# Both mixers' value products in plain float32, two 64-column halves at a time, in bursts

## The chip, the cores and the metric

The kernel runs on one core of one Trainium2 chip. The metric is the device time of one execution in microseconds (us). TensorE (PE) multiplies matrices into PSUM banks of 128 x 512 float32; VectorE (DVE), ScalarE (ACT) and GpSimd (POOL) do the rest, and SyncE (SP) issues most DMAs. Each engine works through its own queue in order.

## The reference, cut to what matters

One layer of a hybrid backbone: 1024 latent tokens and 128 context tokens of width 1024. One projection gives queries, keys, values and gates for two mixers of 8 heads of 64, with 2 key/value groups each. Mixer A attends from every latent token to all 1024 latent and 128 cached context keys. Mixer B attends to a window of +-128 tokens and the cached context, with a sink logit in the softmax. The context tokens attend to themselves.

```python
# mixer A, one block of 128 queries (k_all, v_all: 128 context + 1024 latent)
s = jnp.einsum('bqkgd,bskd->bkgqs', qblk, k_all).astype(jnp.float32) * (d ** -0.5)
p = jax.nn.softmax(s, axis=-1).astype(v_all.dtype)
o = jnp.einsum('bkgqs,bskd->bqkgd', p, v_all)
...
# mixer B: the same over [sink, context, band of three blocks], the sink's weight dropped
o = einsum('bnkgqs,bskd->bnqkgd', p_ctx, v_ctx) + einsum('bnkgqs,bnskd->bnqkgd', p_band, vband)
...
out = jnp.concatenate([o_a * jax.nn.silu(g_a), o_b * jax.nn.silu(g_b)], axis=-1) @ w_out
xs = xs + gate * out
```

Everything is float32. The kernel reaches that accuracy on TensorE by splitting an operand into a high part in the type float32r and a low part (the rest), and adding the products of the parts.

## The kernel before, in words

The first part of the kernel (to about 300 us of the profile) normalises, modulates, projects and stores queries and gates in DRAM; keys and values stay in SBUF. The change touches there only how values are stored: `put_values` casts them to a high part `v_hi`, and `split_values` makes low parts by subtraction.

The rest is attention and the output projection, written as one loop over *slots* (L1365). A unit is (t, m, g): a block of 128 queries, a mixer (m = 0 is A, 1 is B) and a key/value group; its tile holds 4 heads x 128 queries = 512 columns. Units come as A, B, A, B for t = 1 to 8, then four context units (t = 0). A latent A unit has nine blocks of 128 keys, a B unit three or four; each block is one slot. So a *pair* (an A unit and the B unit behind it) has 12 or 13 slots. A context unit has one block and one empty slot. In every slot the program emits, in this order:

- `tick()`: what `later(n, f)` put down n slots before;
- `scores`: for A two products into a bank of tag B, which has two banks (L1217, L1218), an exp on ACT into `pe` (L1220), a cast to the high part `ph` (L1221) and the low part `pl` by subtraction on POOL, for one block in nine on DVE (L1225, L1223). For B the weights are already normalised exps in natural layout; four transposes turn them (L1212), ACT casts the high part (L1213), DVE subtracts (L1214);
- `due` items: the maxima of a later A unit (products L941, reductions on DVE, at most two a slot), and in the first four slots of an A unit the scores of the B unit behind it (L998, L999), a masked minimum with its read-out on DVE (L1002) and an exp on ACT in the next slot (L988). The negated maxima `m_nat` are transposed (L960) and written by DVE into the rows 64 to 67 of `qb` (L961), which L1218 of the next A unit reads;
- in the first four slots of all, 24 late gate products (L1146);
- products of the output projection from the queue `outq` (L1313), as many as the rate allows (`OUTRATE`, a slot); 24 for each latent pair, 36 for each context pair;
- `values` of the block that is `LAG` = 3 slots old: for A three products into the bank `pv`, for B two:

```python
nc.tensor.matmul(pv, two, ph, start=(b == 0), stop=False)                 # L1235
if m == 0:
    nc.tensor.matmul(pv[0:64, :], vl, ph, start=False, stop=False)        # L1237
nc.tensor.matmul(pv, two, pl, start=False, stop=last)                     # L1238
```

`two` is 128 columns wide: 64 columns of high values and, for A, 64 columns of ones, so the softmax's sums land in partitions 64 to 127; for B the second 64 columns are the low values. After a unit's last block, at the slots in `END_AT`, `LAST_END` or `PROMPT_END`, `inverse` makes 1/sum on ACT as exp(-ln) (A) or copies the second half (B, L1247), `gated` multiplies or adds the halves on DVE (two instructions, L1259) and multiplies with the gate `sgl` on POOL (L1261), `parts` splits the result into `ogh` (ACT, L1271) and `ogl`, and behind a B unit the pair's output products join `outq`. For B the gate `sgl` has been multiplied with 1/sum before, on POOL (L1045). `load_gate` fetches a unit's gate two units ahead. `in_order` keeps each engine's instructions in the order in which the program emits them.

Of the kernel before, what the change touches and what calls it, by code (L numbers as in the profile page):

```python
# [36 lines left out]
LAG = 3  # L37
# [93 lines left out]
def hybrid_step(ctx, tc, x_prompt, x_sample, cache_k_a, cache_v_a, cache_k_b, cache_v_b,  # L131
# [631 lines left out]
    v_hi = kv.tile([P, 2, 20, 2, HD], F32R, name="v_hi")  # L763
    v_lo = kv.tile([P, 20, HD], F32R, name="v_lo")
# [7 lines left out]
    def split_values(src, j):  # L772

        nc.vector.tensor_tensor(v_lo[:, j : j + 2, :], src[:, 0], v_hi[:, 0, j : j + 2, 0, :], op=ALU.subtract)
        nc.vector.tensor_tensor(v_hi[:, 1, j : j + 2, 1, :], src[:, 1], v_hi[:, 1, j : j + 2, 0, :], op=ALU.subtract)

    with tc.tile_pool(name="kt", bufs=2) as kt:
        W_GB.pools[WRAW : WRAW + 2] = [(kt, 2)] * 2
        sg_tile.append(lambda n: kt.tile([P, 512], F32, tag="kh", name=n))
        for b in range(0, 20, 4):  # L780
            later(4 + b // 2, lambda b=b: nc.gpsimd.tensor_scalar(
                v_hi[:, 0, b : b + 4, 1, :], gain4, 0.0, 1.0, op0=ALU.mult, op1=ALU.add))
        ones = ident_r.bitcast(F32)[64:68].unsqueeze(1)
        for out, n in ((kla[64:68].rearrange("p g b n -> p (g b) n"), 18), (klp[64:68, 0:2], 2)):
            later(ONES_AT, lambda out=out, n=n: nc.vector.tensor_scalar(
                out, ones.to_broadcast([4, n, P]), 0.0, 1.0, op0=ALU.mult, op1=ALU.add))
# [40 lines left out]
        def put_values(src, t):  # L827
            j = 2 * t if t else 18
            nc.scalar.copy(v_hi[:, :, j : j + 2, 0, :], src)
            later(1, lambda: split_values(src, j))  # L830
# [50 lines left out]
        later(VC_AT, lambda: nc.scalar.copy(v_hi[:, :, 0:2, 0, :], vc))  # L881
        later(VC_AT + 1, lambda: split_values(vc, 0))
# [295 lines left out]
    def blocks(t, m, g):  # L1178

        if t == 0:  # L1180
            k = (khp[:, g, :], klp[0:68, g, :]) if m == 0 else 0
            return [(k, v_hi[:, m, 18 + g], v_lo[:, 18 + g, :])]
        if m == 0:
            return [((kha[:, g, b, :], kla[:, g, b, :]), v_hi[:, 0, 2 * b + g], v_lo[:, 2 * b + g, :]) for b in range(9)]
        p0, p1_ = window(t)
        at = {p: b + 1 for b, p in enumerate(POS)}
        return [(p - p0, v_hi[:, 1, 2 * at.get(p, 0) + g], None) for p in range(p0, p1_)]
# [5 lines left out]
    def load_gate(i):  # L1193
        if i < NU:
            t, m, g = units[i]
            sgl[i] = w2.tile([P, 2, P], F32, tag="sgl", name=f"sgl{i}")
# [4 lines left out]
    def parts_tiles(i, b):  # L1201
        return [w3.tile([P, 512], F32R, tag=n, name=f"{n}{i}_{b}") for n in ("ph", "pl")]

    def scores(i, b, blk):
# [3 lines left out]
        ph, pl = parts_tiles(i, b)  # L1208
        if m == 1:
# [3 lines left out]
            nc.scalar.copy(ph, s)  # L1213
            later(1, lambda: nc.vector.tensor_tensor(pl, s, ph, op=ALU.subtract))  # L1214
            return ph, pl
# [3 lines left out]
        pe = w3.tile([P, 512], F32, tag="pe", name=f"pe{i}_{b}", bufs=PES)  # L1219
        nc.scalar.activation(pe, s, AF.Exp)  # L1220
        nc.scalar.copy(ph, pe)  # L1221
        if (i - PROMPT_AT in PROMPT_PL) if t == 0 else b in PL_DVE:
            later(1, lambda: nc.vector.tensor_tensor(pl, pe, ph, op=ALU.subtract))  # L1223
        else:
            nc.gpsimd.tensor_tensor(pl, pe, ph, op=ALU.subtract)  # L1225
        return ph, pl

    def values(i, b, last, blk, ph, pl):
        t, m, g = units[i]
        _, vh, vl = blk  # L1230
        if b == 0:
            pvb[i] = bank(PROMPT_PV[i - PROMPT_AT] if t == 0 else "C", f"pv{i}")
        pv = pvb[i]
        two = vh.rearrange("p s d -> p (s d)")
        nc.tensor.matmul(pv, two, ph, start=(b == 0), stop=False)  # L1235
        if m == 0:
            nc.tensor.matmul(pv[0:64, :], vl, ph, start=False, stop=False)  # L1237
        nc.tensor.matmul(pv, two, pl, start=False, stop=last)  # L1238
        if not last:
            return  # L1240

        v = {}

        def inverse():
            v["rs"] = w2.tile([64, 512], F32, tag="rs", name=f"rs{i}", bufs=1)
            if m == 1:
                nc.scalar.copy(v["rs"], pv[64:128, :])  # L1247
                return
            nc.scalar.activation(v["rs"], pv[64:128, :], AF.Ln)
            nc.scalar.activation(v["rs"], v["rs"], AF.Exp, scale=-1.0)  # L1250

        def gated():
            rs = v["rs"]
            o = 768 + 256 * (i % 3)
            of = spare[0][:, o : o + 256].rearrange("p (c n) -> p c n", c=2)
            pvv = pv[0:64, :].rearrange("p (c s n) -> p c s n", s=2, n=P)
            srv = rs.rearrange("p (c s n) -> p c s n", s=2, n=P)
            for s in range(2):
                nc.vector.tensor_tensor(of[64 * s : 64 * s + 64], pvv[:, :, s, :], srv[:, :, s, :],  # L1259
                                        op=ALU.add if m else ALU.mult)  # L1260
            nc.gpsimd.tensor_tensor(of, of, sgl.pop(i), op=ALU.mult)  # L1261
            later(GATE_LATE, lambda: load_gate(i + 2))
# [13 lines left out]
        ends = PROMPT_END if t == 0 else END_AT if i < PROMPT_AT - 2 else LAST_END  # L1276
        for n, f in zip(ends, (inverse, gated, parts)):
            later(n, f)
        if m == 1:
            later(ends[3], lambda: outq.extend(out_items(t, g)))  # L1280
# [81 lines left out]
    credit, live = 0.0, []  # L1362
    load_gate(0)
    load_gate(1)
# [86 lines left out]
```

## Time and profile before

| | |
|---|---|
| time, median of 3 runs | 704.2 us (704.17 to 704.34) |
| span of the profiled execution | 704.1 us; the page gives no other time for it |
| PE busy | 691.6 us, 98% |
| DVE, ACT, POOL busy | 443.3, 420.0, 342.3 us |
| mean granted TensorE clock | 0.997 |

In the rows that follow, L-numbers are lines of the kernel. A row of a group of instructions reads: line, engine, operation, out<-in, shapes and count, then busy us and mean ns of one, then idle time of the engine before them and what ended it. A matmul's shape is written rows*columns of the weights, then the moving operand. A row in order of time has its start and length in us first. Lengths of matmuls overlap, because they are pipelined.

### The profile page before, as it was taken

Reading aid. Unit: us, or ns where it says so; the run is one execution under the profiler, and the core shown is the slowest. Engines: PE = TensorE matmul, PEld = TensorE weight load, DVE = VectorE, ACT = ScalarE, POOL = GpSimd, SP = SyncE. Lnnn points to the kernel's source line nnn. Section 1 sums busy time; section 2 is a strip of 40 time slices with the busy share of each in tenths; the row PEclk is TensorE's granted clock in tenths of the full one; section 3 lists DMA queues with packets and bytes.
Section 4 is the critical chain, followed back from the end, with each engine's and each line's share of the span. In section 5 each row is a group of like instructions: output and inputs, shape, how many; then the busy total and the mean of one; then the engine's idle time right before and its main releaser. Section 6 shows DMA issues by size and latency. Waiting matters only on the chain.

```text
span 704.1 us, 10711 instructions
## 1 busy us (share of the span) xinstructions
PE 691.6 (98%) x3554; PEld 561.4 (80%) x3554; DVE 443.3 (63%) x991; ACT 420.0 (60%) x856; POOL 342.3 (49%) x364
## 2 busy tenths in 40 slices
PE   6999999999999999999999999999999999999997
PEld 2788988878788789986788888878888888887876
DVE  3555247875676873537677577667666775775564
ACT  4455411412233553389877877787788778877870
POOL 3457023332323241657857655755574557456742
PEclk9999999999999999999999999999999999999999
DMA  8960283348435015423222122121211231212324
GB/s 330 415 245 16 109 305 76 72 93 295 131 89 175 1 61 187 157 64 102 90 69 83 34 82 73 46 82 58 86 61 52 69 90 46 83 52 90 91 60 144
DMA packets 53447, 78.64 MB, mean 112 GB/s; under 512 B 6848, under 2 KB 25728, under 8 KB 52368
## 3 DMA queue, kind: packets, MB, share of 16 engines
q1 hardware_dynamic: 45360, 66.28, 27.8%
q10 hardware_dynamic: 8032, 11.68, 6.2%
q8 instruction: 28, 0.46, 0.3%
q14 instruction: 27, 0.22, 0.1%
HBM read 58.72 MB, written 19.21 MB: 111 GB/s over the span
## 4 chain that ended last, share of the span: by engine, by line
PE 88%; ACT 4%; DMA 2%; DVE 2%; issue 2%; ACTq 1%; SPq 0%; POOL 0%; DVEq 0%; POOLq 0%
PE po L1313 14%; PE pv L1238 6%; PE pv L1235 6%; PE pmx L941 5%; PE st L1217 4%; PE pv L1237 4%; PE st L1218 4%; PE pq L279 4%; PE pq L280 4%; PE pq L278 4%; PE st L1212 4%; PE pg L292 3%; PE pg L293 3%; PE pg L288 3%; PE pk L279 2%; PE pk L280 2%
## 5 line engine op out<-in xcount | busy, mean ns | idle before, releaser
L1225 POOL TENSOR_TENSOR pl<-pe,ph 128x512 fp32r<-128x512 f32 x130 | 167.9, 1294 | 141.9 <-DVE nm L1002 67.5
L942 DVE TENSOR_REDUCE mx<-pmx 128x1 f32<-128x384 f32 x192 | 101.4, 553 | 57.3 <-PE pmx L941 56.2
L1220 ACT ACTIVATE pe<-st 128x512 f32<-128x512 f32 x146 | 86.7, 594 | 27.1 <-PE st L1218 26.4
L1221 ACT CAST ph<-pe 128x512 fp32r<-128x512 f32 x146 | 90.6, 621 | 4.8
L1238 PE MATMUL pv<-pl,v_hi 128*128 128x512 f32 x208 | 82.5, 397 | 0.3 <-POOL pl L1225 0.3
L1235 PE MATMUL pv<-ph,v_hi 128*128 128x512 f32 x208 | 82.6, 397 | 0.0
L197 POOL TENSOR_TENSOR rs_q<-ms_q,mhalf 128x8 f32<-128x8 f32 x18 | 34.8, 1931 | 80.7 <-DVE ms_q L195 80.7
L1313 PE MATMUL po<-wo,ogh 128*128 128x512 f32 (+1 forms) x224 | 73.1, 387 | 0.0
L1002 DVE CUSTOM_DVE_ANT_0 sn<-sn,mask,nsink 128x512 f32<-128x512 f32 (+1 forms) x64 | 46.4, 724 | 41.0 <-PE sn L999 38.6
L941 PE MATMUL pmx<-kha,qt 128*128 128x384 f32 x192 | 61.0, 363 | 0.5 <-ACT pen L988 0.3
L1217 PE MATMUL st<-qt,kha 128*128 128x512 f32 x144 | 57.9, 402 | 0.1
L1237 PE MATMUL pv<-ph,v_lo 128*64 128x512 f32 x146 | 57.6, 395 | 0.0
L1218 PE MATMUL st<-qb,kla 68*128 68x512 f32 x144 | 57.1, 397 | 0.0
L1238 PEld LDWEIGHTS pv<-pl,v_hi 128*128 128x128 f32 x208 | 39.2, 188 | 17.3 <-POOL pl L1225 0.7
L988 ACT ACTIVATE pen<-sn,nm 128x512 f32<-128x512 f32 (+2 forms) x72 | 44.9, 625 | 5.8 <-DVE nm L1015 2.7
L1213 ACT CAST ph<-st 128x512 fp32r<-128x512 f32 x62 | 36.4, 587 | 19.7 <-PE st L1212 19.4
L1313 PEld LDWEIGHTS po<-wo,ogh 128*128 128x128 f32 x224 | 41.0, 188 | 6.2 <-ACT ogh L1271 0.3
L1235 PEld LDWEIGHTS pv<-ph,v_hi 128*128 128x128 f32 x208 | 39.3, 189 | 7.0 <-issue 0.3
L1313 PE MATMUL po<-wo,ogl 128*128 128x512 f32 (+1 forms) x112 | 43.2, 386 | 0.0
L1214 DVE TENSOR_TENSOR pl<-st,ph 128x512 fp32r<-128x512 f32 x62 | 42.4, 685 | 1.2 <-ACT ph L1213 0.7
L675 ACT ACTIVATE sqq<-pq 128x512 f32<-128x512 f32 x18 | 10.8, 598 | 53.3 <-PE pq L280 13.8
L941 PEld LDWEIGHTS pmx<-kha,qt 128*128 128x128 f32 x192 | 35.5, 190 | 6.4 <-DVE mx L942 1.2
(238 smaller groups left out, 1701.3 us busy)
## 6 DMA issues: line engine op xcount, KB each, us to landing
qt<-qd SPq DMA_DIRECT2D x36, 256.0 KB
wm<-in_w_mod_ss_dram SPq DMA_DIRECT2D x8, 1024.0 KB
qd<-qo0q ACTq DMA_DIRECT2D x36, 128.0 KB
qd<-qo1q ACTq DMA_DIRECT2D x36, 128.0 KB
sgl<-gd SPq DMA_DIRECT2D x36, 128.0 KB
out_dram<-yt SPq DMA_DIRECT2D x17, 256.0 KB
xn<-in_x_sample_dram SPq DMA_DIRECT2D x8, 512.0 KB
wg<-in_w_mod_g_dram SPq DMA_DIRECT2D x4, 1024.0 KB
```

The source lines that it names most:

```text
L941: nc.tensor.matmul(pm[:, 0:384], lhs, kha[:, g, 3 * b : 3 * b + 3, :], start=True, stop=True)
L942: nc.vector.tensor_reduce(mx[:, h, b : b + 1], pm[:, 0:384], axis=AX.X, op=ALU.max)
L1002: nc.vector.tensor_tensor_reduce(s, s, mask[:, m0 : m0 + n], -1.0, nsink[:, 4 * g + h : 4 * g + h + 1], op0=ALU.add, op1=ALU.min, accum_ou ...
L1217: nc.tensor.matmul(s, kh, qtile[i], start=True, stop=False)
L1218: nc.tensor.matmul(s, kl, qbtile[i], start=False, stop=True)
L1220: nc.scalar.activation(pe, s, AF.Exp)
L1221: nc.scalar.copy(ph, pe)
L1225: nc.gpsimd.tensor_tensor(pl, pe, ph, op=ALU.subtract)
L1235: nc.tensor.matmul(pv, two, ph, start=(b == 0), stop=False)
L1237: nc.tensor.matmul(pv[0:64, :], vl, ph, start=False, stop=False)
L1238: nc.tensor.matmul(pv, two, pl, start=False, stop=last)
L1313: nc.tensor.matmul(po[c], x, wo_parts[KT * n + k][lo][:, q], start=(k == KS[0] and p == 0), stop=(k == KS[-1] and p == 2))
```

## The change

Values are kept once, as plain float32 (`v_all`, 64 columns a block), and the weights `pe` stay plain float32 as well: the casts to `ph`, the low parts `pl`, `v_lo` and the value splits go. A values product is now a pair: the same 64 columns of values as weights, once against the 256 columns of the even heads into the partitions 0 to 63, once against those of the odd heads into 64 to 127, both in columns 0 to 255 of `pv`. For A, POOL adds up the unit's nine `pe` tiles in `acc`, and one more pair with a 128 x 64 tile of ones puts the sums into columns 256 to 511. The result lies as the gate does, so `rs` is 128 x 256, POOL multiplies the gate with it (A), and DVE does one multiplication of `pv` with the gate.

Products are no longer emitted block by block. When the sixth block of a latent A unit is `LAG` = 2 slots old, the pairs of blocks 0 to 5 are emitted (first burst); when the last block of the B unit is 2 slots old, A's other three, A's sums and all of B's (second burst). A context pair has one burst. `pe` has 12 buffers instead of 3, the gates are loaded four units ahead, `pv` of context units is always of tag C, the ends come 1, 3, 4 (A) and 2, 3, 6 slots (B) after the second burst, and `OUTRATE` is 2.0 instead of 2.5.

```diff
-LAG = 3
+LAG = 2
...
-OUTRATE = 2.5
+OUTRATE = 2.0
...
-PES = 3
+PES = 12
+SPLIT = 6
 GATE_LATE = 2
-END_AT = (1, 4, 6, 9)
-PROMPT_END = (2, 4, 5, 7)
+ENDS = ((1, 3, 4), (1, 2, 3, 6))
...
-    v_hi = kv.tile([P, 2, 20, 2, HD], F32R, name="v_hi")
-    v_lo = kv.tile([P, 20, HD], F32R, name="v_lo")
+    v_all = kv.tile([P, 2, 20, HD], F32, name="v_all")
+    ones = kv.tile([P, HD], F32, name="ones")
+    nc.gpsimd.memset(ones, 1.0)
...
             for h in range(4):
                 nc.tensor.transpose(s[:, P * h : P * h + P], penat[i][:, h, o : o + P], ident_r.bitcast(F32))
-            nc.scalar.copy(ph, s)
-            later(1, lambda: nc.vector.tensor_tensor(pl, s, ph, op=ALU.subtract))
-            return ph, pl
+            nc.scalar.copy(pe, s)
+            return pe
...
         nc.scalar.activation(pe, s, AF.Exp)
-        nc.scalar.copy(ph, pe)
-        if (i - PROMPT_AT in PROMPT_PL) if t == 0 else b in PL_DVE:
-            later(1, lambda: nc.vector.tensor_tensor(pl, pe, ph, op=ALU.subtract))
+        if b == 0:
+            acc[i] = pe
         else:
-            nc.gpsimd.tensor_tensor(pl, pe, ph, op=ALU.subtract)
-        return ph, pl
+            first = acc[i]
+            if b == 1:
+                acc[i] = w3.tile([P, 512], F32, tag="acc", name=f"acc{i}", bufs=2)
+            nc.gpsimd.tensor_tensor(acc[i], first, pe, op=ALU.add)
+        return pe
+
+    def values(i, made, first, last):
...
+        def product(o, lhs, rhs, start, stop):
+            r = rhs.rearrange("p (c s n) -> p c s n", s=2, n=P)
+            for s in range(2):
+                nc.tensor.matmul(pv[HD * s : HD * s + HD, o : o + 256].rearrange("p (c n) -> p c n", c=2), lhs,
+                                 r[:, :, s, :], start=start, stop=stop)
+
+        n = len(made)
+        for b, (blk, pe) in enumerate(made):
+            product(0, blk[1], pe, first and b == 0, m == 1 and b == n - 1)
         if not last:
             return
+        if m == 0:
+            product(256, ones, acc.pop(i), False, True)
...
         def inverse():
-            v["rs"] = w2.tile([64, 512], F32, tag="rs", name=f"rs{i}", bufs=1)
             if m == 1:
-                nc.scalar.copy(v["rs"], pv[64:128, :])
                 return
-            nc.scalar.activation(v["rs"], pv[64:128, :], AF.Ln)
-            nc.scalar.activation(v["rs"], v["rs"], AF.Exp, scale=-1.0)
+            rs = w2.tile([P, 256], F32, tag="rs", name=f"rs{i}")
+            nc.scalar.activation(rs, pv[:, 256:512], AF.Ln)
+            nc.scalar.activation(rs, rs, AF.Exp, scale=-1.0)
+            sg = sgl[i]
+            later(1, lambda: nc.gpsimd.tensor_tensor(sg, sg, rs.rearrange("p (c n) -> p c n", c=2), op=ALU.mult))
...
+            nc.vector.tensor_tensor(of, pv[:, 0:256].rearrange("p (c n) -> p c n", c=2), sgl.pop(i), op=ALU.mult)
+            later(GATE_LATE, lambda: load_gate(i + 4))
...
+        if s < len(slots) and slots[s]:
+            i, b, last, blk = slots[s]
+            live.setdefault(i, []).append((blk, scores(i, b, blk)))
+            if last and units[i][1] == 1:
+                ready[s + LAG] = [(i - 1, not units[i][0], True), (i, True, True)]
+            elif units[i][1] == 0 and b == SPLIT - 1 and units[i][0]:
+                ready[s + LAG] = [(i, True, False)]
...
-        if s >= LAG and live:
-            slot, parts = live.pop(0)
-            if slot:
-                values(*slot, *parts)
+        if s in ready:
+            for j, first, whole in ready.pop(s):
+                values(j, live.pop(j), first, whole)
```

More of the change, by code (lines that the diff above doesn't have):

```diff
@@ L1229, in values @@
+        return pe
+    def values(i, made, first, last):
         t, m, g = units[i]
[L1230 to L1232 removed]
+        if first:
+            pvb[i] = bank("C", f"pv{i}")
         pv = pvb[i]
[L1234 to L1237, printed above, removed]
```

60 lines of the change are left out of this document (19 added, 41 removed).

## The prediction

> **What bounds the kernel now.** I read the page first (busy times, slices, chain), then one steady stretch, then rows in order of time.
>
> ```profile
> PE 691.6 (98%) x3554; PEld 561.4 (80%) x3554; DVE 443.3 (63%) x991; ACT 420.0 (60%) x856; POOL 342.3 (49%) x364
> ...
> PE   6999999999999999999999999999999999999997
> ...
> PE 88%; ACT 4%; DMA 2%; DVE 2%; issue 2%; ACTq 1%; SPq 0%; POOL 0%; DVEq 0%; POOLq 0%
> ```
> ```profile
> 506.66:530.53 23.87, 23.87 (x117) 19.18 (x116) 17.68 (x37) 18.73 (x37) 14.09 (x15) 1.00 0.26 84
> ```
>
> TensorE (PE) is busy from the second slice to the last, and the chain of waits is 88% PE. The second fence is one steady pair of units (nine A slots and four B slots), from one m_nat transpose to the next. Its columns are length, then busy time of PE, PEld, DVE, ACT and POOL, then granted clock, DMA share and GB/s. PE fills all 23.87 us at clock 1.00, and nobody else exceeds 18.73. So a step counts by the time for which it holds PE. Busy durations overstate that time; it is read from starts:
>
> ```profile
> 517.16 0.34 PE L941 MATMUL pmx<-kha,qt 128*128 128x384 f32 x1
> 517.33 0.62 PE L1313 MATMUL po<-wo,ogh 128*128 128x512 f32 x2
> 517.79 0.39 PE L1235 MATMUL pv<-ph,v_hi 128*128 128x512 f32 x1
> 518.02 0.39 PE L1237 MATMUL pv<-ph,v_lo 128*64 128x512 f32 x1
> 518.25 0.39 PE L1238 MATMUL pv<-pl,v_hi 128*128 128x512 f32 x1
> 518.48 0.40 PE L1217 MATMUL st<-qt,kha 128*128 128x512 f32 x1
> ```
> ```profile
> L1235 PE MATMUL pv<-ph,v_hi 128*128 128x512 f32 x208 | 82.6, 397 | 0.0
> L1238 PE MATMUL pv<-pl,v_hi 128*128 128x512 f32 x208 | 82.5, 397 | 0.3 <-POOL pl L1225 0.3
> ...
> L1237 PE MATMUL pv<-ph,v_lo 128*64 128x512 f32 x146 | 57.6, 395 | 0.0
> ```
>
> Each values product records 0.39 us but starts 0.23 after the one before (0.233 over the pair's 35); a maximum product (L941) takes 0.17. **Removed from PE:** 208 + 208 + 146 = 562 products x 0.233 = 130.9 us.
>
> **The new products.** A plain-float32 product with narrow weights stands twice in the trace, on 32 columns. In each, four column strips work side by side:
>
> ```profile
> 155.08 0.39 PE L280 MATMUL pq<-whiqb,h 128*128 128x512 f32 x1
> 155.40 1.92 PE L651 MATMUL pgate<-wg,sil32g 128*32 128x512 f32 x16
> 157.25 0.66 PE L703 MATMUL ptq<-ident_r,qfq 128*128 128x128 f32 x4
> ```
> ```profile
> 155.85 0.13 PEld L651 LDWEIGHTS pgate<-wg,sil32g 128*32 128x32 f32 x4 [0.30 <-issue]
> 156.28 0.13 PEld L651 LDWEIGHTS pgate<-wg,sil32g 128*32 128x32 f32 x4 [0.30 <-issue]
> ```
> ```profile
> 31.24 0.38 PE L426 MATMUL px<-ident,xn 128*128 128x128 f32 x2
> 31.55 1.07 PE L375 MATMUL pm<-wm,sil 128*32 128x256 f32 x16
> 32.55 0.50 PE L292 MATMUL pg_f<-h,whiga 128*128 128x512 f32 x1
> 32.88 0.39 PE L293 MATMUL pg_f<-h,wloga 128*128 128x512 f32 x1
> ```
>
> Eight products of the code (L651, one call) are 16 records: float32 goes through twice. The weight loads come in fours, 0.43 apart (155.85, 156.28): a round is four strips of 512 columns in 0.43 us, so 256 columns take 0.215. L375 has 256 columns: 16 records, three rounds between first and last start, (1.07 - 0.40)/3 = 0.22. A pair of the change is two 64-wide strips of 256 columns, each twice: two rounds if the strips overlap, 2 x 0.216 = 0.432 us. If they don't, four rounds, 0.863. Four strips overlap in these rows; I take 0.432 and keep the other end as a rival.
>
> **Added to PE:** 146 A blocks, 62 B blocks and 18 sums = 226 pairs x 0.432 = 97.6 us.
>
> **Entering and leaving a burst.** From 31.24 to 32.88 are 1.64 us: two transposes at 0.11, four rounds (0.86) and one gate product (0.23) make 1.31, so the change into strips and back costs 0.33. The L651 rows bound it below: 157.25 - 155.08 = 2.17, less 0.23 and four rounds of 0.43, is 0.22. Behind a burst of the change stands an fp32r score product, as L292 stands behind L375: 0.33. There are two bursts in each of 16 latent pairs and one in each of two context pairs: 34 x 0.33 = 11.2 (7.5 by the lower bound).
>
> PE work: -130.9 + 97.6 + 11.2 = **-22.1 us**, about 1.45 a steady pair.
>
> **What it takes off other engines.**
>
> ```profile
> L1221 ACT CAST ph<-pe 128x512 fp32r<-128x512 f32 x146 | 90.6, 621 | 4.8
> L1220 ACT ACTIVATE pe<-st 128x512 f32<-128x512 f32 x146 | 86.7, 594 | 27.1 <-PE st L1218 26.4
> ...
> L988 ACT ACTIVATE pen<-sn,nm 128x512 f32<-128x512 f32 x48 | 32.9, 685 | 3.2 <-DVE nm L1002 2.4
> L1271 ACT CAST ogh<-spare 128x256 fp32r<-128x256 f32 x36 | 14.5, 402 | 2.3 <-POOL spare L1261 2.2
> ...
> L1247 ACT COPY rs<-pv 64x512 f32<-64x512 f32 x18 | 10.5, 583 | 1.1 <-PE po L1313 0.7
> ```
> ```profile
> L1225 POOL TENSOR_TENSOR pl<-pe,ph 128x512 fp32r<-128x512 f32 x130 | 167.9, 1294 | 141.9 <-DVE nm L1002 67.5 <-ACT ph L1221 60.7 <-POOL pl L1225 11.2
> ```
> ```profile
> L1214 DVE TENSOR_TENSOR pl<-st,ph 128x512 fp32r<-128x512 f32 x62 | 42.4, 685 | 1.2 <-ACT ph L1213 0.7
> ```
>
> A pair leaves ACT at 18.73 - 9 x 0.621 = 13.1, DVE at 17.68 - 5 x 0.685 = 14.3, POOL at 14.1 (eight 1.29 us additions for eight subtractions; one gate multiplication moves ahead of DVE). PE's values products waited 0.3 us for POOL in all, so these are zero by themselves. Zero as well, with their cover: the shorter lag (the last B copy, 0.59, has a whole A slot of 1.4 before the burst); the 12 pe buffers (one is written again 12 slots on, five or more behind the burst that frees it); the gating (outputs need it five slots on); two more gate loads ahead on SP and the value splits in the key stage (PE is full there in the slices); the lower output rate, which moves the same products.
>
> **Where PE can starve.** Values work leaves 11 of 13 slots, so there a slot is its scores, maxima and two output products. I follow ACT after the second burst, in slots 2 to 7 of the next A:
>
> ```profile
> 508.78 0.39 PE L1218 MATMUL st<-qb,kla 68*128 68x512 f32 x1
> ...
> 509.21 0.60 ACT L1220 ACTIVATE pe<-st 128x512 f32<-128x512 f32 x1 [0.48 <-PE st L1218]
> 509.25 0.39 PE L999 MATMUL sn<-klb,qt 128*128 128x512 f32 x1
> ...
> 509.68 0.76 DVE L1002 CUSTOM_DVE_ANT_0 sn<-sn,mask,nsink 128x512 f32<-128x512 f32 x1 [0.23 <-PE sn L999]
> ...
> 510.53 0.69 ACT L988 ACTIVATE pen<-sn,nm 128x512 f32<-128x512 f32 x1
> ...
> 511.21 0.59 ACT L1220 ACTIVATE pe<-st 128x512 f32<-128x512 f32 x1
> ```
>
> An exp starts 0.43 after its second score product starts, a masked weight's exp 1.28 after its own (510.53 - 509.25). Put the burst's end at 0. Leaving strips puts the first score product at 0.11 (32.55 against a last round that ends at 32.44) and the second at 0.45 (0.33 later, as 32.88). Exp 2 starts at 0.88, ends 1.48. The masked exp waits until 2.20 and ends 2.88, exp 3 ends 3.47, an ogh cast 3.87, the last masked exp 4.55, exp 4 5.15, the other ogh cast 5.55, exp 5 **6.15**. PE in the same slots: four scores slots with two output products each (4 x 4 x 0.233), masked products in two (4 x 0.233), three maxima (0.17 each), one slot with scores alone (0.47), and the 0.22 of leaving strips: it wants scores 7 at **5.87**. Scores have two banks, so scores 7 waits for exp 5: 0.3 us. The ends: 0 if the masked exp comes early, 0.7 if both read-outs behind these exps count in full. I take 0.3, what the chain gives: 14 steady pairs, **+4.2** (0 to 9.8).
>
> In the first latent pairs there are no output products yet, 4 slots x 0.47 = 1.9 us less cover; the 24 late gate products cover the first pair, not the second: **+2** (0 to 4).
>
> The prompt units at the end:
>
> ```profile
> 674.92 0.31 PE L1011 MATMUL sn<-khp,qt 128*128 128x128 f32 x1
> ...
> 681.25 0.60 PE L1212 MATMUL st<-ident_r,pen 128*128 128x128 f32 x4
> ```
>
> From mixer B's context scores to the transposes of its weights are 6.3 us, some 5.7 without the copy of B's sums that stands in ACT's queue. The outputs of the last latent block now start two slots sooner and are used up; PE has 0.9 of scores (eight of 128 columns, 0.11 each as the transposes), 0.9 of outputs, 0.6 of the next A and a three-pair burst of 1.6: 4.0 against 5.7. **+1.5** (0 to 3).
>
> One wait I expect not to move:
>
> ```profile
> 506.66 0.22 PE L960 MATMUL ptm<-ident_r,m_nat 128*4 128x128 f32 x1
> 506.72 0.60 PE L1212 MATMUL st<-ident_r,pen 128*128 128x128 f32 x4
> ...
> 506.92 0.68 DVE L961 TENSOR_TENSOR qb<-ptm,diag 4x512 fp32r<-4x512 f32 x1 [0.36 <-PE ptm L960]
> ```
>
> qb is ready 0.94 after ptm starts. Its first reader came at 508.78, 2.12 later; without the two values products between it comes 1.4 to 1.6 later, still behind.
>
> **Sum.** The profiled execution has a span of 704.1 and the median is 704.2: 704.1 - 22.1 + 4.2 + 2 + 1.5 = **689.7 us**. Low: lower burst price, no starving, 704.1 - 22.1 - 3.7 = 678. High: 704.1 - 22.1 + 9.8 + 4 + 3 = 699.
>
> **Rivals.**
> 1. *Slower: the two halves run one behind the other.* Only four-strip products on 32 columns are in the trace, none on 64 (L1237 is 64 wide, but alone and fp32r). Then 226 x 0.431 = 97.4 more on PE, which covers the starving: 704.1 + 75.3 = 779. It decides from a pair price of (130.9 - 11.2)/226 = 0.53 on. Against it: rounds of four. 0.07.
> 2. *Weight loads come out from behind the products.* Each of 452 rounds would show a load of some 0.11 to 0.13 (the 155.85 row): 452 x 0.11 = 50, so 740. In the rows the loads of a round run while the round before streams, and its 0.43 holds. 0.03. The Trainium skill says so ("TensorE: Matmul & The Clock Gate", Part 3, What overlaps and what doesn't): a weight load overlaps products in flight only where its row group differs; both halves use all rows, so by that rule this rival would hold. The L651 strips use all rows as well and hide their loads, so this trace disagrees.
> 3. *PE starves oftener.* DVE's two reductions in a slot, POOL's additions behind DVE and the ACT chain together cost over 0.7 a pair: 699 to 703, and no gain from 22.1/16 = 1.4 a pair on. Every engine's sum a pair (13 to 14 above) is far under 22.4, so only locally. 0.14, of it 0.02 within 0.2% and 0.03 slower.
> 4. *Bursts cheaper, chain covered:* 672 to 678. 0.06.
>
> **How the numbers follow.** The forecast (678 to 699) has 0.70. The range 676 to 702 takes in most of rival 3 and some of 4. A measurement here tells about 0.2%, 1.4 us. Faster: 0.70 + 0.09 + 0.06 = 0.85; same 0.02; slower 0.07 + 0.03 + 0.03 = 0.13.
>
> **What the profile after would show.** The values line: 904 records, starts of both halves within 0.02 us, rounds 0.216; if the halves' starts alternate, rival 1. Around a burst 0.33. A steady pair at 22.4 to 23.1 us; over that, PE's idle time names ACT's exp of scores (mine) or DVE (rival 3). The ACT casts gone; POOL's count unchanged in kind.

## The result, and the profile after

The changed kernel takes 693.67 us (median of four runs, 693.26 to 694.89) against 704.23 (704.17 to 704.34) for the kernel before, run beside it: a ratio of 0.9853, 95% interval 0.9839 to 0.9867, so 1.5% faster. The forecast was 689.7 in a range of 676 to 702. The profiled execution of the changed kernel took 694.89 us, the longest of its four, with a span of 693.0 and a mean granted clock of 0.994 (the other three 0.998); that matters below.

From the page after: busy times, the slices of PE and of its granted clock, the chain, and two groups of section 5.

```profile
PE 675.0 (97%) x3896; PEld 522.8 (75%) x3896; DVE 374.3 (54%) x857; ACT 309.0 (45%) x692; POOL 323.3 (47%) x340
...
PE   6999999999999999998999999999999999999997
...
PEclk9999999999999999999899999999999999999999
...
PE 87%; DMA 4%; DVE 3%; ACT 2%; issue 1%; POOL 1%; ACTq 1%; SPq 1%; DVEq 0%; POOLq 0%
...
L1215 POOL TENSOR_TENSOR acc<-acc,pe 128x512 f32<-128x512 f32 x112 | 143.5, 1281 | 37.8 <-ACT pe L1208 35.4
...
L1228 PE MATMUL pv<-pe,v_all 128*64 128x256 f32 x832 | 101.6, 387 | 0.0
```

PE is still what bounds the kernel. ACT and DVE have lost 111 and 69 us, while the time fell by 10.6. New are two eights among the slices, one in PE's busy share (312 to 329 us) and, just behind it, one in the clock (329 to 347 us). Both belong to the second pair.

The two bursts of steady pairs, the second burst first, PE's rows in order of time (start, length, then the group):

```profile
505.58 0.39 PE L1305 MATMUL po<-wo,ogh 128*128 128x512 f32 x1
505.90 0.65 PE L1228 MATMUL pv<-pe,v_all 128*64 128x256 f32 x4
506.38 0.60 PE L1228 MATMUL pv<-acc,ones 128*64 128x256 f32 x4
506.81 1.90 PE L1228 MATMUL pv<-pe,v_all 128*64 128x256 f32 x16
508.64 0.51 PE L1206 MATMUL st<-qt,kha 128*128 128x512 f32 x1
508.98 0.39 PE L1207 MATMUL st<-qb,kla 68*128 68x512 f32 x1
...
515.34 0.63 PE L1305 MATMUL po<-wo,ogh 128*128 128x512 f32 x2
515.90 3.67 PE L1228 MATMUL pv<-pe,v_all 128*64 128x256 f32 x32
519.50 0.50 PE L1206 MATMUL st<-qt,kha 128*128 128x512 f32 x1
```

Sixteen records of the second burst are eight rounds of two halves, seven steps between first and last start: (1.90 - 0.39)/7 = 0.216 us a round. So the two 64-column halves run side by side, and a pair costs 0.432. The text ahead of the prediction is wrong in one point: the first burst has 32 records, eight pairs and not six. It starts two slots behind A's sixth block and takes all blocks that have been scored by then. The second burst has one A block (4 records), the sums (4) and four B blocks (16).

Stretches from one transposition of the negated maxima to the next, steady pair first (length, then busy time of PE, PEld, DVE, ACT and POOL, granted clock, DMA share, GB/s), from the windows view of the changed kernel:

```profile
501.81:524.58 22.77, 22.76 (x136) 16.66 (x136) 13.56 (x31) 11.73 (x27) 13.29 (x14) 1.00 0.22 72
```
```profile
300.22:340.93 40.71, 38.03 (x209) 27.17 (x207) 16.33 (x42) 23.06 (x52) 26.76 (x27) 0.92 0.29 95
340.93:365.22 24.29, 22.90 (x134) 16.83 (x135) 12.30 (x28) 13.07 (x29) 16.73 (x17) 1.00 0.24 74
```
The same two stretches of the kernel before:
```profile
301.79:338.81 37.02, 36.23 (x174) 27.74 (x173) 20.98 (x50) 34.05 (x71) 26.95 (x28) 1.00 0.31 97
338.81:363.49 24.68, 24.68 (x120) 19.69 (x119) 16.68 (x35) 19.42 (x39) 18.13 (x19) 1.00 0.20 61
```

| stretch, us | before | after | difference | the prediction's terms give |
|---|---|---|---|---|
| up to the transposition with which attention starts | 301.8 | 300.2 | -1.6 | 0 |
| first two latent pairs | 37.02 | 40.71 | **+3.7** | -0.8 |
| third pair | 24.68 | 24.29 | -0.4 | -1.15 |
| eleven steady pairs | 262.5 | 250.4 | -12.0 | -12.6 |
| last two latent pairs, context units, tail | 78.1 | 77.4 | -0.7 | +0.2 |

So the steady pairs did what was forecast, and what is missing was lost at the start of attention. The waits view of the changed kernel, PE alone, 300 to 640 us (us in total, times, longest), says on what:

```profile
PE pmx L932 <- ACT pen L979: 3.1, 3, 1.4
PE pmx L932 <- DVE mx L933: 0.5, 1, 0.5
PE st L1206 <- ACT pe L1208: 0.2, 1, 0.2
```

The one of 1.4 us in the second pair, in order of time with all engines:

```profile
324.54 0.73 POOL L1036 TENSOR_TENSOR sgl<-sgl,spare 128x256 f32<-128x256 f32 x1
...
325.23 0.73 POOL L1248 TENSOR_TENSOR sgl<-sgl,rs 128x256 f32<-128x256 f32 x1
325.30 0.40 PE L1207 MATMUL st<-qb,kla 68*128 68x512 f32 x1
325.30 0.42 DVE L1254 TENSOR_TENSOR spare<-pv,sgl 128x256 f32<-128x256 f32 x1 [1.59 <-POOL sgl L1036]
325.64 0.62 DVE L993 CUSTOM_DVE_ANT_0 sn<-sn,mask,nsink 128x384 f32<-128x384 f32 x1
...
326.35 0.58 ACT L979 ACTIVATE pen<-sn,nm 128x384 f32<-128x384 f32 x1 [0.19 <-DVE nm L993]
...
327.08 1.01 PE L932 MATMUL pmx<-kha,qt 128*128 128x384 f32 x2 [1.38 <-ACT pen L979]
```

Read from the bottom: PE stood 1.38 us for a bank of tag A, which has two banks for the maxima and for B's scores, and which B's masked weights still held; their exp waited for DVE's masked minimum (L993); DVE stood 1.59 us with the minimum behind a multiplication with the gate (L1254); and that waited for POOL (L1036), which multiplies B's gate with its 1/sum (`later(ROWS_AT[3], ...)`) behind two of its 1.28 us additions. Behind a 12-slot pair this multiplication and DVE's gating are emitted in the same slot; behind a 13-slot pair it is a slot earlier. The same chain returns in the third and in the last latent pair, which also follow 12-slot pairs. In the last one DVE stands 1.61 us for L1036, and PE 0.86 for a bank of the scores. In the third pair PE stands 1.38, but DVE waits only 0.63 for POOL and also does a split of output weights there (L1093, 1.34 us).

### The profile page after: what moved, and what is told of

It reads as the page before. It is cut to its first block, busy times and chain, and to the rows that moved or that the text cites. A ratio compares the mean times of both kernels' runs of the same rounds, so it can differ in the third digit from the quotient of the medians.

```text
span 693.0 us, 10923 instructions
## 1 busy us (share of the span) xinstructions
PE 675.0 (97%) x3896; PEld 522.8 (75%) x3896; DVE 374.3 (54%) x857; ACT 309.0 (45%) x692; POOL 323.3 (47%) x340
## 4 chain that ended last, share of the span: by engine, by line
PE 87%; DMA 4%; DVE 3%; ACT 2%; issue 1%; POOL 1%; ACTq 1%; SPq 1%; DVEq 0%; POOLq 0%
PE pv L1228 14%; PE po L1305 14%; PE st L1206 5%; PE pmx L932 5%; PE st L1207 4%; PE pq L279 4%; PE pq L280 4%; PE pq L278 4%; PE st L1202 4%; PE pg L288 3%; PE pg L292 3%; PE pg L293 3%; PE pk L279 2%; PE pk L280 2%; PE pk L278 2%; DMA wm<-in_w_mod_ss_dram 2%
## 5 line engine op out<-in xcount | busy, mean ns | idle before, releaser
L1215 POOL TENSOR_TENSOR acc<-acc,pe 128x512 f32<-128x512 f32 x112 | 143.5, 1281 | 37.8 <-ACT pe L1208 35.4
L1228 PE MATMUL pv<-pe,v_all 128*64 128x256 f32 x832 | 101.6, 387 | 0.0
L1228 PEld LDWEIGHTS pv<-pe,v_all 128*64 128x64 f32 x832 | 57.3, 138 | 38.3 <-issue 8.4
L993 DVE CUSTOM_DVE_ANT_0 sn<-sn,mask,nsink 128x512 f32<-128x512 f32 (+1 forms) x64 | 46.3, 724 | 68.6 <-PE sn L990 67.9
L1215 POOL TENSOR_TENSOR acc<-pe,pe 128x512 f32<-128x512 f32 x16 | 20.4, 1276 | 96.2 <-ACT pe L1208 73.9
L1206 PE MATMUL st<-qt,kha 128*128 128x512 f32 x144 | 61.4, 426 | 1.2 <-ACT pe L1208 1.1
L1203 ACT COPY pe<-st 128x512 f32<-128x512 f32 x62 | 36.4, 587 | 32.9 <-PE st L1202 32.9
L1206 PEld LDWEIGHTS st<-qt,kha 128*128 128x128 f32 x144 | 27.2, 189 | 20.9 <-issue 8.5
L1202 PE MATMUL st<-ident_r,pen 128*128 128x128 f32 x248 | 37.5, 274 | 1.1 <-DVE pen L1030 1.1
L441 POOL TENSOR_TENSOR h<-hf,h 128x256 fp32r<-128x256 f32 (+2 forms) x33 | 28.0, 862 | 20.7 <-DVE h L440 20.7
L1202 PEld LDWEIGHTS st<-ident_r,pen 128*128 128x128 f32 x248 | 29.2, 141 | 7.5 <-ACT ogh L1264 1.5
```

Source lines behind the costliest of these rows:

```text
L993: nc.vector.tensor_tensor_reduce(s, s, mask[:, m0 : m0 + n], -1.0, nsink[:, 4 * g + h : 4 * g + h + 1], op0=ALU.add, op1=ALU.min, accum_ou ...
L1202: nc.tensor.transpose(s[:, P * h : P * h + P], penat[i][:, h, o : o + P], ident_r.bitcast(F32))
L1206: nc.tensor.matmul(s, kh, qtile[i], start=True, stop=False)
L1215: nc.gpsimd.tensor_tensor(acc[i], first, pe, op=ALU.add)
L1228: nc.tensor.matmul(pv[HD * s : HD * s + HD, o : o + 256].rearrange("p (c n) -> p c n", c=2), lhs, r[:, :, s, :], start=start, stop=stop)
```

## The experiments

All edits are to the changed kernel unless said otherwise. Ratios are to the kernel before, run beside each.

**E1: B's gate multiplication one slot earlier.**
```diff
-ROWS_AT = (1, 1, 4, 6)
+ROWS_AT = (1, 1, 4, 5)
```


> One number changed against the changed kernel (693.7 us): mixer B's gate is multiplied with 1/sum on POOL one slot sooner. Theory 1: behind a pair of 12 slots that multiplication is emitted in the very slot in which DVE gates B; POOL has two additions before it, DVE waits for POOL, the masked minimum waits behind on DVE, the exp on ACT, and PE finds no free bank for a maximum product: idle 1.4 us in pair 2, 1.4 us in pair 3, 1.0 us in pair 16. In pair 2 the idle time is followed by 6.7 us at a granted clock of 0.51, which costs another 3.2 us. With the multiplication one slot sooner all three waits and the low clock go: 686 to 688 us. Theory 2 (the one predicted): the first pairs starve because no output products run beside them; then nothing changes, 693 to 694 us.

694.58 us (693.82 to 696.92), ratio 0.9865 [0.9842, 0.9888]: no gain, where theory 1 said 686 to 688. Yet the first two pairs fell from 40.71 to 36.92, the stall of the second pair to 0.57 (now behind a reduction of DVE), and the clock stayed at 1.00. The time went elsewhere: every second steady pair rose to 23.2 to 23.6. There POOL waits for the load of 1/sum, issued one slot ahead, on a queue where a store of the output stands before it. E1's waits of POOL (408 to 432 us) and its SP queue:

```profile
POOL sgl L1036 <- DMA spare<-rd: 9.6, 1, 9.6
```
```profile
411.20 0.34 SPq L1312 DMA_DIRECT2D out_dram<-yt  x1
411.63 1.32 SPq L1050 DMA_DIRECT2D spare<-rd  x2
```

So the cause of the stall in the second pair is confirmed, and the cure put POOL, with the additions behind it, behind a DMA.

**E6: the load one slot earlier too.**
```diff
-ROWS_AT = (1, 1, 4, 6)
+ROWS_AT = (1, 1, 3, 5)
```


> As the run with the gate one slot sooner, but the load of 1/sum (two DMAs on SP) is also issued one slot sooner, before the output store that stands ahead of it in every second pair. Theory: in the run before, POOL waited for that load in every second pair (9.6 us in one pair, the additions behind it) and DVE's reductions came late, 0.85 us for each of these pairs, which ate what the first pairs won. With both sooner, the first pairs keep the gain and the steady pairs stay at 22.75: 688 to 690 us. Rival: the load then waits on SP for the store of 1/sum and blocks the loads behind it; no gain, 693 us or more.

689.06 us (688.91 to 690.68), ratio 0.9782 [0.9767, 0.9798], the fastest of all. First two pairs 36.95, third 23.58, steady pairs 22.76, the last latent pair 18.85 (20.07 in the changed kernel). The 4.6 us gained by the medians come from the stalls and the clock behind them; the steady pairs are unchanged. (The expectations of E10 and E12 call these two steps the gate steps of A and B; both are B's: the load and the multiplication.)

**E7: the multiplication one slot earlier behind 12-slot pairs alone.**
```diff
-            later(ROWS_AT[3], lambda: ...
+            later(ROWS_AT[3] - (t in (1, NL)), lambda: ...
```


> The gate multiplication one slot sooner only where the pair has 12 slots (t = 1 and 8), all others as changed. If the waits in pairs 2, 3 and 16 come from the multiplication standing in the same slot as DVE's gating, they shrink as in the run with all of them sooner (1.6 to 0.7 and 1.0 to 0.5), the low clock goes, and the steady pairs stay at 22.75: 688 to 690 us. If the steady pairs became slower for another reason, still 22.75 here but no gain at the start: 692 to 694 us.

690.45 us (690.06 to 690.97), ratio 0.9797 [0.9783, 0.9812]; first two pairs 37.0, steady 22.76. E1's gain without its loss: this one slot was the stall of the second pair (1.38 before, 0.62 now). In the third pair 1.17 of 1.38 us is left, where less was expected: L1093 takes 1.83 us of DVE there.

**E2: six products without use in slot 17, ahead of the maxima.** Their result is not read.
```diff
+FILL_AT, FILL = 17, 6
...
+        if s == FILL_AT:
+            fill = bank("D", "fill")
+            for _ in range(FILL):
+                nc.tensor.matmul(fill, kha[:, 0, 0, :], qtile[slots[s][0]], start=True, stop=True)
```


> The changed kernel with six idle fp32r products of 512 columns (6 x 0.23 = 1.4 us, into a bank that nobody uses then) put before the two maximum products of slot 17, where PE idles 1.4 us. The wait stays and its time is filled. Theory 1: the idle time brings the low clock, so the clock stays at 1.00 and 3 us are won, 690 to 691 us, with the maximum products no earlier. Rival: the low clock comes from elsewhere (power, another unit's work) and stays: 693 to 695 us.

692.12 us (691.79 to 692.72), ratio 0.9824 [0.981, 0.9839]; first two pairs 38.12. More work on PE and less time. By the medians the gain is 1.6 us and not the 3 expected: that price was read from the profiled execution of the changed kernel, and its other three lost less clock. The windows view, changed kernel, then E2:

```profile
321.00:327.00 6.00, 4.32 (x21) 2.52 (x17) 2.38 (x7) 3.80 (x12) 5.29 (x6) 0.98 0.36 129
327.00:333.80 6.80, 6.72 (x24) 4.58 (x26) 2.11 (x5) 2.60 (x7) 6.24 (x9) 0.51 0.53 173
```
```profile
321.00:327.00 6.00, 5.62 (x28) 3.63 (x23) 2.44 (x7) 3.83 (x12) 5.31 (x6) 1.00 0.41 137
327.00:333.80 6.80, 6.74 (x44) 4.21 (x45) 2.04 (x4) 2.29 (x6) 6.28 (x9) 1.00 0.53 166
```

Behind the idle time the granted clock of the changed kernel is 0.51 for 6.8 us, in which PE does 24 products instead of 44. With PE kept busy it stays at 1.00, in all four executions of E2.

**E3: the two halves' lists one behind the other** (all products of the even heads, then all of the odd heads).
```diff
-        for b, (blk, pe) in enumerate(made):
-            product(0, blk[1], pe, ...)        # both halves
+        for s in range(2):
+            for b, (blk, pe) in enumerate(made):
+                product(0, blk[1], pe, ..., s)
```


> In each burst all products of the low half are emitted, then all of the high half, so that neighbours stand on the same 64 columns of the array. If the gain is that two halves stream side by side, each product takes its two passes alone: 226 x 0.43 = 97 us more, less what starving it covers: 780 to 792 us. If TensorE itself moves products of the other half ahead, or the halves never overlapped, no change: 693 to 695 us.

747.5 us (one run), 53.8 more than the changed kernel, not 97. The burst of eight pairs in E3, to set against 515.90 above:

```profile
518.20 6.31 PE L1228 MATMUL pv<-pe,v_all 128*64 128x256 f32 x32
```

Between first and last start 5.92 us instead of 3.28. Thirty-two records one at a time would need 31 steps of 0.216, 6.70; four steps are missing. In the single records the first twelve start 0.216 apart, the next eight in four rounds of two, the last twelve alone again: the last four of the first half run beside the first four of the second (a record does not name its half; this is read from the starts). The second burst shows the same four (its B lists, eight records a half, run four alone, four rounds of two, four alone; its A lists, four records a half, run side by side throughout). That is twelve rounds more in the first burst and four in the second, 16 x 0.216 = 3.5 us a pair, and steady pairs take 26.32 instead of 22.77. So the order of the halves does decide, as rival 1 feared, and at a junction of lists PE runs four records of each beside one another, no more: that is why E3 costs 54 us and not 97.

**E4: values by block again**, each block's pair in its own slot.
```diff
+            ready.setdefault(s + LAG, []).append((i, b == 0, last and units[i][1] == 1))
...
-                values(j, live.pop(j), first, whole)
+                values(j, [live[j].pop(0)] if live[j] else [], first, whole)
```


> No bursts: each block's pair is emitted when the block is two slots old, A's sums with the last B block. 34 bursts become 208 (16 x 13 - 4 latent, 4 context). If each entry and exit costs 0.36 us as the rows around the bursts say: 174 x 0.36 = 63 us more, 750 to 757 us. If the cost is only that of the first round and the first score product behind (0.15): 26 us more, 720 us.

762.52 us (one run), 68.9 more. More than the 750 to 757 expected. A burst's entry and exit cost 0.35 where scores follow, 0.30 before transposes. E4 also waits for DVE's gating, 20.4 us in all, and its clock was halved for 13.7 us, so the price of a burst cannot be read from the total alone:

```profile
PE pv L1228 <- DVE spare L1254: 11.4, 8, 3.3
PE pv L1228 <- DVE of L1254: 9.0, 8, 3.1
```

**E8: one burst a pair of units** (15 weight buffers).
```diff
-PES = 12
+PES = 15
...
-            elif units[i][1] == 0 and b == SPLIT - 1 and units[i][0]:
-                ready[s + LAG] = [(i, True, False)]
```


> One burst a pair: all of A, the sums and B together, two slots after the pair's last scores, with 15 pe buffers for 12. 16 bursts fewer at 0.36 us: 5.7 us less, 688 us, if nothing starves. Rival: between bursts 12 slots pass with no values work, ACT's exps have no long burst halfway to catch up, and PE waits for the score banks, 0.3 to 1 us a pair: 693 to 704 us.

710.0 us (709.44 to 712.12), ratio 1.0082 [1.0059, 1.0104]. Slower than the rival's 693 to 704 too. Sixteen bursts at 0.35 are saved (5.6 us), and yet steady pairs rise from 22.77 to 23.89. Most of it is that A's output now ends with B's and PE waits for it, 0.6 to 1.0 us a pair:

```profile
PE po L1305 <- POOL ogl L1267: 11.3, 14, 1.3
```

Just ahead of it, as the rival has it, PE also waits for ACT's exp of scores (0.14 us at 523.03) and for a reduction of DVE (0.27 at 524.05).

**E11: a first burst of really six blocks.**
```diff
-                values(j, live.pop(j), first, whole)
+                made = live[j] if whole else live[j][:SPLIT]
+                live[j] = live[j][len(made):]
+                values(j, made, first, whole)
```


> The changed kernel with a first burst of really six blocks (the trace of the changed kernel has eight pairs in it), so bursts of 6 and 8 pairs for a 13-slot pair instead of 8 and 6. Theory 1 (a burst costs 0.36 for entering and leaving, however long it is): the same number of bursts, the same products, 693.7 within 1.4. Theory 2 (the longer second burst stands just ahead of the next unit's scores and gives the exps more time, or holds the weights' buffers longer): steady pairs move by 0.1 us or more in one direction, 1.4 us or more in all.

693.83 us (693.49 to 695.37), ratio 0.9852 [0.9837, 0.9867]: no difference, and the steady pairs stay at 22.74 to 22.77.

**E5: the old output rate in the changed kernel.**
```diff
-OUTRATE = 2.0
+OUTRATE = 2.5
```


> The changed kernel with the old output rate, 2.5 instead of 2.0 products a slot: that part of the change undone alone. If PE's work sets the time, the same products only move: within 1 us of 693.7. If the even rate matters because each slot without products (now two or three in a row, before 7 of a pair) leaves PE waiting for ACT or DVE: 2 to 6 us more.

714.47 us (714.05 to 715.41), ratio 1.014 [1.0124, 1.0155]. With the rate alone taken back, the change makes the kernel slower, by far more than the 2 to 6 us expected. Steady pairs alternate between 25.2 and 23.7. Waits of PE in E5, and a place where the outputs have run out:

```profile
PE pmx L932 <- ACT pen L979: 5.6, 14, 1.4
PE pmx L932 <- DVE mx L933: 5.2, 7, 0.8
PE st L1207 <- DVE qb L952: 4.0, 6, 0.7
```
```profile
475.13 0.34 PE L932 MATMUL pmx<-kha,qt 128*128 128x384 f32 x1
475.30 0.48 PE L1206 MATMUL st<-qt,kha 128*128 128x512 f32 x1
475.62 0.39 PE L1207 MATMUL st<-qb,kla 68*128 68x512 f32 x1
476.25 0.45 PE L932 MATMUL pmx<-kha,qt 128*128 128x384 f32 x1 [0.25 <-ACT pen L979]
```

Neither values nor outputs are left in these slots; scores and maxima come as fast as PE can issue them and stand for ACT and DVE.

**E9: the new rate in the kernel before.**
```diff
-OUTRATE = 2.5
+OUTRATE = 2.0
```


> The kernel before with the output rate of the change (2.0 a slot instead of 2.5), nothing else. Theory 1 (the rate is worth its 20.8 us only where values leave most slots empty): in the kernel before each slot holds two or three values products of 0.233, PE has no idle time to fill, so 704.2 within 1.4 us, and a steady pair stays at 23.8 to 23.9. Theory 2 (the rate is a gain by itself, that the change only took along): 2 us or more faster, below 702, and then the gain of the change is not that of the values products. A slower run, above 705.6, would say that outputs that are spread out come late for the next pair.

708.97 us (708.85 to 709.21), ratio 1.0063 [1.0047, 1.008]: slower by 4.7 us. Neither theory holds; it is the third outcome named, but the outputs are not late for the next pair. A steady pair takes 24.27 on average instead of 23.87. One of the new gaps, all engines:

```profile
528.80 0.68 DVE L1214 TENSOR_TENSOR pl<-st,ph 128x512 fp32r<-128x512 f32 x1
...
529.62 0.63 PE L1212 MATMUL st<-ident_r,pen 128*128 128x128 f32 x4
```

PE's last product before started at 529.15; the transposes follow 0.47 later instead of 0.23, once DVE has read B's score bank for the low parts. DVE came to that late, behind the read-outs of output products that now run to the pair's end (L1318 at 527.47, L1319 at 528.19 in the same view). A second gap of 0.21, at the scores that start at 509.05, stands as close behind another such subtraction (508.21 to 508.90). The change removes the subtraction. That it removes this cost of an even rate with it is read from these rows; no run takes the subtraction away alone.

**E10: E6, and the weights of mixer B's context units (scores, exps, division) begun six slots ahead instead of four.** (The expectation says that the negated maxima are transposed earlier; the edit moves these weights.)
```diff
-PROMPT_LEAD = 4
+PROMPT_LEAD = 6
```


> The changed kernel with the gate step of mixer A one slot sooner and that of B one slot sooner (as in the fastest run so far, 689.06), and with the negated maxima of the context units transposed six slots ahead instead of four. Theory 1 (the 1.33 us that the last transposes waited, at 670.21 in the changed kernel, are the missing cover of the context units): the stretch from the last but one to the last of them and the tail lose 1.0 to 1.3 together, 687.7 to 688.2. Theory 2 (the context units end on the chain of exps, casts and outputs behind them, not on that wait): the wait goes, the tail grows by as much, 689.1 within 0.5.

689.62 us (689.2 to 689.73), ratio 0.9787 [0.9773, 0.9802]: no gain, the time of theory 2. The wait of 1.1 us ahead of the transposes of these weights (L1202 at 664.21 in E6, 670.21 in the changed kernel) is gone. But 1.2 us are lost ahead of it, at 652.86, where the context units' exps now hold the bank that the transposition of the last latent B unit's 1/sum needs (E10, waits of PE, 630 to 690 us):

```profile
PE pti L1040 <- ACT pen L979: 1.2, 1, 1.2
```

**E12: E6 with an output rate of 1.85.**
```diff
-OUTRATE = 2.0
+OUTRATE = 1.85
```


> The changed kernel with the gate step of mixers A and B one slot sooner (689.06 alone) and an output rate of 1.85 a slot, 24 products over 13 slots, instead of 2.0. In the changed kernel the last slot of a steady pair has one output product fewer than the others, and the maxima transposes there stand 0.41 behind the product before them instead of 0.23. Theory 1 (that hole, 0.18 a pair, goes when output products reach to the pair's end): steady pairs of 22.55 to 22.65 instead of 22.76, some 2 us in all, 686.5 to 688. Theory 2 (the last output products then come behind the next pair's first maxima, and DVE's read-outs of them stand ahead of its reductions; a 12-slot pair hands two products on): steady pairs unchanged or up, 689 to 692.

696.98 us (695.29 to 697.09), ratio 0.9896 [0.988, 0.9913]: 7.9 us over E6, and outside both theories (686.5 to 688, 689 to 692). Steady pairs are at 23.0 to 23.5 instead of 22.76. The hole ahead of the maxima's transposition (0.17 in E6) stays in five of eleven steady pairs, shrinks to 0.10 in three and grows to 0.41 in three, so theory 1 falls. The rest stands at one maxima product, the first of the fourth slot behind the second burst (513.14 in the changed kernel):

```profile
533.04 0.44 PE L932 MATMUL pmx<-kha,qt 128*128 128x384 f32 x1 [0.38 <-ACT pen L979]
```

In E6 it starts 4.8 us behind the last product of that burst, with six output products between, and PE waits 0.03. In nine of the eleven pairs of E12 only five stand between; it still starts 4.8 us behind the burst (once 5.1), and PE waits 0.22 to 0.26 for ACT or DVE (once 0.54). In the two pairs with six it waits 0.03. So the work on ACT and DVE behind a burst has a length of its own, and the lower rate takes away a product that covered it. The last latent pair takes 21.64 instead of 18.85; PE waits 1.8 us of that for a low part on POOL (L1267).

## Why the prediction was right, and where it was off

- **The price of a pair.** 0.432 was taken from 32-column strips; the 64-column halves measure 0.216 a round. Rival 1 (halves one behind the other) and rival 2 (weight loads exposed) fall. E3 shows that rival 1's mechanism is real and that the order of emission keeps it away. The rule that the Trainium skill states ("TensorE: Matmul & The Clock Gate", Part 3, What overlaps and what doesn't) and that stood beside rival 2 does not hold in these rows: both halves use all rows, and with 832 loads the rounds stay at 0.216.
- **A burst.** 0.33 predicted; over 29 bursts of the changed kernel the way in and out cost 0.35 each (products at 0.233, rounds at 0.216). On 34 bursts that is +0.7 us. The term itself is needed: the 515.90 burst starts 0.33 behind an output product instead of 0.23, and the scores behind it are 0.34 apart.
- **Steady starving.** The size was right, the cause only in part. A pair of 23.87, less 35 products of 0.233, plus 14 pairs of 0.432 and two bursts of 0.35, makes 22.46; it took 22.77, so 0.31 is lost, 0.3 was forecast. But no row shows PE waiting there for ACT's fifth exp. The loss stands in two other places, in every steady pair (changed kernel; the loads of the weights name what PE waited for):

```profile
410.32 0.40 PE L1305 MATMUL po<-wo,ogh 128*128 128x512 f32 x1
410.73 0.08 PEld L951 LDWEIGHTS ptm<-ident_r,m_nat 128*4 128x4 f32 x1 [0.45 <-DVE mx L933]
...
513.14 0.30 PEld L932 LDWEIGHTS pmx<-kha,qt 128*128 128x128 f32 x2 [0.30 <-ACT pen L979]
```

The transposition of the maxima starts 0.41 behind the output product instead of 0.23: 0.18, for a reduction of DVE, which is rival 3's mechanism at a quarter of the 0.7 a pair that rival 3 needed. The maxima product of 513.14 starts 0.26 behind the score product ahead of it instead of 0.23, and the next one 0.28 behind it instead of 0.17: 0.14, for the exp of B's masked weights, whose scores hold the bank. That is the ACT chain of the prediction, but it ends at a bank of the maxima, ahead of the score bank that the prediction watched. E12 bears out the second: with one output product (0.23) less in front of it the wait grows by as much. No run took the reductions away.
- **First pairs: the term that was mis-sized.** "+2 (0 to 4)" came from cover that is missing while there are no output products. With the work saved it gave -0.8 for two pairs; they lost 3.7. The prediction's first line of zeros held the cause: "one gate multiplication moves ahead of DVE". It was costed by POOL's sum over a pair. In its place in the queue it stands behind two additions, and DVE, ACT and PE stand behind it. E1, E6 and E7 show this for the second pair; E2 shows that 2.6 us of it are the clock in the profiled execution (1.6 by the medians), since it leaves the wait and only keeps PE busy through it. With the stall gone (E6) the two pairs take 36.95, 0.1 less than before, so what else they lose is some 2.7 of the 2.8 saved: that is within the term's range, and the stall with its clock came on top of it.
- **The lower output rate: not zero.** It was costed at nothing, as a step "which moves the same products". The sum came out only because the change brings the rate along: it is what keeps PE covered in the eleven slots that values leave. E5 puts its worth at 20.8 us in the changed kernel (714.47 against 693.67), and E9 shows that it costs 4.7 in the kernel before. That the sum held without this is luck: with the old rate the same sum would have been 25 us off. In E5 the wait for `qb`, which the prediction did not expect to move, becomes real too (4.0 us).
- **Context units.** A hole of 1.5 was forecast; a wait of 1.1 is there, ahead of the transposes of B's context weights, as forecast. E10 shows that starting their chain two slots earlier takes this wait away and brings one of 1.2 ahead of it.
- **The base.** The sum was set against a span of 704.1. Other executions of the same kernel have spans of 702.0 to 703.9 at times of 703.8 to 705.7, some 1.8 us less than the time. The profiled execution reached attention 1.6 us later than the changed kernel's, where PE does the same work, because its clock was down for 3.4 us near the start (windows view of the kernel before):

```profile
16.76:20.18 3.42, 3.42 (x23) 2.61 (x16) 0.72 (x2) 0.62 (x2) 0.73 (x1) 0.50 1.00 404
```

So the base was 1.6 us late, and 1.8 us outside the span were left out; that the two cancel is luck.

## To carry to other kernels

When work leaves a bound engine, ask what still fills each slot of it: here 22 us of products were saved, and without spreading other products evenly into the space the kernel would have been slower than before (E5: 20.8 us). An instruction that moves to another engine is costed at its place in that engine's queue, with all that waits behind it, not by the engine's sum. And a stall in a thin stretch of TensorE can be paid twice, once as idle time and once as clock.

## What was not expected of the hardware

**The clock after 1.4 us of idle time.** Five profiled executions have the 1.4 us stall in the second pair: in four (the changed kernel, E5, E8, E11) the clock fell behind it, in E3 it did not. In E4 PE stood there 3.3 us, behind another wait, and the clock fell. In the six in which PE idled there for 0.62 or less at a time (E1, E2, E6, E7, E10, E12) it stayed at 1.00. The same stall in the third pair cost no clock.

What tells the cases apart is how much of the idle time falls into one stretch of a fixed grid. In every profiled execution the stretches of one granted clock are whole multiples of 3.41 us long (in the changed kernel 94, then 2 at half clock, then 105), apart from the last, which the end of the execution cuts off. Laid on this grid, PE's busy time ahead of the fall in the changed kernel and E8, and in the two stretches that came near and cost nothing, the changed kernel's third pair and E3:

```profile
323.41:326.82 3.41, 1.91 (x7) 0.79 (x5) 1.82 (x7) 2.03 (x5) 3.41 (x4) 1.00 0.41 155
```
```profile
325.84:329.25 3.41, 1.98 (x7) 0.89 (x6) 2.31 (x7) 2.36 (x7) 2.93 (x4) 1.00 0.21 61
```
```profile
350.71:354.12 3.41, 2.03 (x10) 1.47 (x9) 2.21 (x6) 2.10 (x7) 2.71 (x4) 1.00 0.17 50
```
```profile
329.02:332.43 3.41, 2.23 (x9) 1.50 (x10) 2.18 (x7) 2.40 (x8) 2.94 (x5) 1.00 0.56 168
```

In E3 the grid cuts the idle time in two. Over the 14 profiled executions, 23 stretches at full clock have PE busy for less than 2.0 of 3.41 us, and 19 of them are followed by half clock; of the 2819 fuller ones none is. So the line lies near 2.0 of 3.41 us, as the profile counts busy time. That busy time is the cause is read from these counts; E2 alone changes it and little else (3.35 us busy in the stretch of the stall, no fall).

A fall costs one or two stretches at half clock, 1.7 or 3.4 us. The clock came back after a stretch with PE busy for 3.39 to 3.41 us (E5, E8, E11); in the changed kernel the first was 3.15, and a second followed. This fits the times: its profiled run is 1.1 to 1.6 us over its other three. The Trainium skill ("TensorE: Matmul & The Clock Gate", Part 1) describes a free-running window of some 3.4 us after whose idleness the clock is halved; the half and the 3.4 us agree with these rows. The Trainium skill's advice (the same page, Why this matters for your kernels) to avoid idle gaps of over about 3 us would have let this one pass: the gap was 1.4 us, in a stretch where PE was busy for 1.91 of 3.41.

**Looking ahead across halves.** In E3, PE overlaps only four records on each side of the junction of two lists. Side by side means written side by side.
